# HGRN2 chunk scores: merging two blocks at a time in seven levels in place of four in three

## The chip, the cores and the metric

The kernel runs on one core of a Trainium2 chip. Its engines work side by side, each through its own queue of instructions in a fixed order, and wait for one another by semaphores: TensorE (PE, matrix products, with PEld for the loading of weights), VectorE (DVE, elementwise work), ScalarE (ACT), GpSimd (POOL) and SyncE (SP, which issues the DMAs here). The metric is the device time of one execution in microseconds (us), lower is better. The kernel before takes 2606.49 us, the median of three runs (2604.78 to 2610.13).

## The reference, cut to what matters

The program is a trunk of two layers over 1024 tokens of width 1024: an HGRN2 mixer, a SwiGLU feed-forward, a dilated attention mixer, a second feed-forward, each with a norm and a residual sum, all in float32. The change is in the HGRN2 mixer, in the scores within a chunk. Per head (8 of them, 128 keys each) and chunk the reference computes

```
b      = cumsum(log f, along the chunk)
decay  = exp(where(s <= t, b[t] - b[s], -inf))          # product of f over s+1 .. t
scores = einsum('bhtk,bhsk,bhtsk->bhts', q, k, decay)   # k = 1 - f
o_t    = (q * exp(b)) @ state + scores @ v
state  = exp(b_last) * state + (k * exp(b_last - b)).T @ v
```

The decay depends on t, s and the key, so the scores are not one matrix product of q and k. The kernel takes chunks of 128 tokens and builds the scores from blocks that grow: between two neighbouring blocks, decay splits into a factor of the query (product of f from its block's start up to t) and a factor of the key (product of f behind s up to its block's end), so that q and k, scaled with these, give that block of scores by a plain product. After each step q and k take up the factor of the block they now belong to.

## The kernel before, in words

All tiles have 128 partitions. A head's q, f and k lie with the key index on the partitions and the 1024 tokens along the row, as eight chunks of 128. A projection "unit" (line 130) loads a 128x1024 weight tile, splits it into a high and a low part (ACT copies, line 108, DVE subtracts, line 109), and multiplies both with the split input v in 48 matmuls of 512 columns (lines 124, 125, 127). Each head has four units: f, q, i, g. The loop over heads (near line 423) issues for head j: f and q, the tail of head j-1, i and g, then `hgrn_scores`, then `hgrn_state`, which transposes values and keys (lines 370, 379), carries the state over the chunks (lines 385, 389) and forms the outputs (lines 395, 397). `hgrn_tail` transposes the result back (line 415) and gates it. For the last head the g unit is issued behind the scores.

`hgrn_scores` (line 273) does three things.

- The diagonal (lines 277 to 287): GpSimd multiplies q and k (line 280); `column_sums` (line 265) splits the product and sums it over the partitions by two matmuls with a matrix of ones; DVE writes that, times the identity, to the score tile `at` (line 282). Then `qp` becomes q times f (line 287).
- Three stages with block sizes m of 1, 4 and 16 (`STAGES`, line 29), each in two halves of 512 tokens. Each merges four blocks into one: ACT and DVE form, in `mb`, the six scaled copies of the queries that the six pairs of blocks need (lines 307 to 309); the products follow (for m = 1 through GpSimd multiplies, line 317, and `column_sums`; for 4 and 16 by matmuls of 192 columns, line 327); DVE forms the block products of f (lines 328 to 330), rescales `qp` and `kk` in place (lines 332 to 336), and writes the three diagonals of blocks into `at` by predicated copies under a mask from `lm` (line 342), twelve to a stage.
- A last merge of two blocks of 64 (lines 346 to 361), by matmuls of 128 columns (line 350) and a predicated copy (line 357).

The order of instructions on each engine is set when the program is built: a scheduler interleaves the independent pieces by its own estimates, so that the matmuls of the next head's f and q units stand between the score matmuls of this head. On the chip each engine runs its list in that order. Score results go to four PSUM buffers (`axps`), unit results to four others (`mmps`). A float32 matmul (both operands F32) shows in the profile as two MATMUL instructions, each with its own LDWEIGHTS; one of F32R operands shows as one.

Of the kernel before, what the change touches and what calls it, by code (L numbers as in the profile page):

```python
# [8 lines left out]
F32 = mybir.dt.float32  # L9
F32R = mybir.dt.float32r  # L10
U8 = mybir.dt.uint8
# [4 lines left out]
P = 128  # L16
T = 1024
D = 1024
KT = D // P
# [9 lines left out]
STAGES = (1, 4, 16)  # L29
NMASK = 3 * len(STAGES) + 1  # L30
EPS = 1e-6
# [4 lines left out]
K_ID, K_BAND, K_DIAG, K_COS, K_SIN, K_LM = 0, 128, 384, 512, 1536, 2560  # L36
# [4 lines left out]
def trunk_kernel(ctx, tc, x, cols, consts, w_in, w_hout, w_qkv, w_aout, w_ffn, w_down, out):  # L41
    nc = tc.nc
    cp = ctx.enter_context(tc.tile_pool(name="cp", bufs=1))
# [7 lines left out]
    def big(tag, name, dt=F32):  # L51
        return gp.tile([P, T], dt, tag=tag, name=name, bufs=slots[tag])
# [7 lines left out]
    def axps(name):  # L60
        return pax.tile([P, 512], F32, tag="ax", name=name)

    def hs(hh):
        return slice(hh * 512, hh * 512 + 512)

    def cs(c):
        return slice(c * P, c * P + P)

# [9 lines left out]
    for k in range(KT):  # L78
        t = big("vc", f"x{k}")
# [16 lines left out]
    ones = cp.tile([P, P], F32, name="ones")  # L96
    nc.vector.memset(ones[:], 1.0)
    onesr = cp.tile([P, P], F32R, name="onesr")
    nc.vector.tensor_copy(onesr[:], ones[:])
# [117 lines left out]
    lm = cp.tile([P, NMASK, 2, P], U8, name="lm")  # L217
    for i0 in range(0, NMASK, 8):
        n = min(8, NMASK - i0)
        lmf = big("ws", f"lmf{i0}")  # L220
        nc.sync.dma_start(lmf[:, 0:n * P], consts[:, K_LM + i0 * P:K_LM + (i0 + n) * P])
        for r in range(2):
            nc.vector.tensor_copy(lm[:, i0:i0 + n, r, :], lmf[:, 0:n * P].rearrange("p (i t) -> p i t", i=n))
# [42 lines left out]
    def column_sums(ps, src, hi, lo):  # L266
        nc.scalar.copy(hi, src)
        nc.vector.tensor_sub(lo, src, hi.bitcast(F32))
        nc.tensor.matmul(ps, onesr[:], hi, start=True, stop=False)
        nc.tensor.matmul(ps, onesr[:], lo, start=False, stop=True)  # L270

    def hgrn_scores(j, f, kk, q):
        at = big("ws", f"at{j}")
        qp = big("ws", f"qp{j}")
        tl = big("ws", f"tl{j}")
        for hh in range(2):
            h0 = hh * 512
            ps = axps(f"dg{j}{hh}")
            pr = big("vb", f"pr{j}{hh}", F32R)
            nc.gpsimd.tensor_mul(qp[:, hs(hh)], q[:, hs(hh)], kk[:, hs(hh)])  # L280
            column_sums(ps[:], qp[:, hs(hh)], pr[:, 0:512], pr[:, 512:T])
            nc.vector.tensor_mul(
                at[:, hs(hh)].rearrange("p (c t) -> p c t", c=4),
                ps.rearrange("p (c t) -> p c t", c=4),
                ident.unsqueeze(1).to_broadcast([P, 4, P]),
            )
            nc.vector.tensor_mul(qp[:, hs(hh)], q[:, hs(hh)], f[:, hs(hh)])
        def blocks(ap, n, m):
            return ap.rearrange("p (g b m) -> p g b m", b=n, m=m)

        space = iter([(tl, 0), (f, 0), (f, 256)])
        tot = f[:]
        for si, m in enumerate(STAGES):
            base, at0 = next(space)
            ng = T // (4 * m)
            tt_all = base[:, at0:at0 + 3 * ng].rearrange("p (g b) -> p g b", b=3)
            nxt = base[:, at0 + 3 * ng:at0 + 4 * ng]
            for hh in range(2):
                n2 = ng // 2
                gs = slice(hh * n2, hh * n2 + n2)  # L300
                mb = big("vb", f"mb{j}_{m}_{hh}")
                tv = tot.rearrange("p (g b) -> p g b", b=4)[:, gs, :]
                tt = tt_all[:, gs, :]
                qv = blocks(qp[:, hs(hh)], 4, m)
                kv = blocks(kk[:, hs(hh)], 4, m)
                mv = blocks(mb[:, 0:768], 6, m)
                nc.scalar.copy(mv[:, :, 0:3, :], qv[:, :, 1:4, :])
                nc.vector.tensor_mul(mv[:, :, 3:5, :], qv[:, :, 2:4, :], tv[:, :, 1:3].unsqueeze(3).to_broadcast([P, n2, 2, m]))
                nc.vector.tensor_mul(mv[:, :, 5, :], mv[:, :, 4, :], tv[:, :, 1:2].to_broadcast([P, n2, m]))
                pss = []  # L310
                if m == 1:
                    xp = big("vb", f"xp{j}_{hh}")
                    yh = big("vb", f"yh{j}_{hh}", F32R)
                    yl = big("vb", f"yl{j}_{hh}", F32R)
                    xv = blocks(xp[:, 0:768], 6, m)
                    for a, n in ((0, 3), (3, 2), (5, 1)):
                        nc.gpsimd.tensor_mul(xv[:, :, a:a + n, :], mv[:, :, a:a + n, :], kv[:, :, 0:n, :])
                for b in range(2):
                    ps = axps(f"lv{j}_{m}_{hh}_{b}")
                    pss.append(ps)  # L320
                    if m == 1:
                        sl = slice(b * 384, b * 384 + 384)
                        column_sums(ps[:, 0:384], xp[:, sl], yh[:, sl], yl[:, sl])
                        continue
                    for c in range(2):
                        c4 = 2 * b + c
                        nc.tensor.matmul(ps[:, c * 192:c * 192 + 192], kk[:, hh * 512 + c4 * P:hh * 512 + c4 * P + P], mb[:, c4 * 192:c4 * 192 + 192], start=True, stop=True)  # L327
                nc.vector.tensor_mul(tt[:, :, 1], tv[:, :, 2], tv[:, :, 3])
                nc.vector.tensor_mul(tt[:, :, 0], tv[:, :, 1], tt[:, :, 1])
                nc.vector.tensor_mul(nxt[:, gs], tv[:, :, 0], tt[:, :, 0])  # L330
                t0 = tv[:, :, 0:1].to_broadcast([P, n2, m])
                nc.vector.tensor_mul(qv[:, :, 1, :], qv[:, :, 1, :], t0)
                nc.vector.tensor_mul(qv[:, :, 2, :], mv[:, :, 3, :], t0)
                nc.vector.tensor_mul(qv[:, :, 3, :], mv[:, :, 5, :], t0)
                nc.vector.tensor_mul(kv[:, :, 0:2, :], kv[:, :, 0:2, :], tt[:, :, 0:2].unsqueeze(3).to_broadcast([P, n2, 2, m]))
                nc.vector.tensor_mul(kv[:, :, 2, :], kv[:, :, 2, :], tv[:, :, 3:4].to_broadcast([P, n2, m]))
                for b in range(2):
                    av = blocks(at[:, hh * 512 + b * 256:hh * 512 + b * 256 + 256], 4, m)
                    pv = blocks(pss[b][:, 0:384], 6, m)
                    for d, s0 in ((1, 0), (2, 3), (3, 5)):  # L340
                        mk = blocks(lm[:, 3 * si + d - 1].rearrange("p r t -> p (r t)"), 4, m)
                        nc.vector.copy_predicated(av[:, :, d:4, :], mk[:, :, d:4, :], pv[:, :, s0:s0 + 4 - d, :])  # L342
            tot = nxt
        tv = tot.rearrange("p (g b) -> p g b", b=2)
        nxt = f[:, 320:328]
        for hh in range(2):
            ps = axps(f"lw{j}_{hh}")
            for c in range(4):
                s = slice(hh * 512 + c * P, hh * 512 + c * P + P)
                nc.tensor.matmul(ps[:, cs(c)], kk[:, s], qp[:, s], start=True, stop=True)  # L350
            kv = blocks(kk[:, hs(hh)], 2, 64)
            qv = blocks(qp[:, hs(hh)], 2, 64)
            gs = slice(4 * hh, 4 * hh + 4)
            nc.vector.tensor_mul(kv[:, :, 0, :], kv[:, :, 0, :], tv[:, gs, 1:2].to_broadcast([P, 4, 64]))
            nc.vector.tensor_mul(qv[:, :, 1, :], qv[:, :, 1, :], tv[:, gs, 0:1].to_broadcast([P, 4, 64]))
            nc.vector.tensor_mul(nxt[:, gs], tv[:, gs, 0], tv[:, gs, 1])
            nc.vector.copy_predicated(
                at[:, hs(hh)].rearrange("p (c t) -> p c t", c=4),
                lm[:, NMASK - 1, 0].unsqueeze(1).to_broadcast([P, 4, P]),
                ps.rearrange("p (c t) -> p c t", c=4),  # L360
            )
        tot = nxt
        return kk, qp, at, tot
# [57 lines left out]
    for j in range(H):  # L421
        f, kk, q = hgrn_fq(j)
        if pend is not None:
            os_.append(hgrn_tail(*pend))
        if j == H - 1:
            vt = scaled(unit(w_in[2 * H + j], v, f"i{j}"), "wx", f"i{j}")
            sc = hgrn_scores(j, f, kk, q)
            g = gated(j, 3 * H, "g")
        else:
            vt, g = hgrn_ig(j)  # L430
# [335 lines left out]
    for j in range(4):  # L766
        st = sp.tile([P, 3, 8, 2], F32, tag="st", name=f"st{j}", bufs=2)
        os3 = []
        for gi in range(3):
            blocks, place = attn_scores(j, gi, st)  # L770
# [124 lines left out]
```

## Time and profile before

| | before |
|---|---|
| median of 3 runs | 2606.49 us (2604.78 to 2610.13) |
| profiled execution, first to last instruction (span) | 2605.1 us; the page gives no other time of this execution |
| PE busy | 2546.4 us, 98% |
| PEld busy | 2118.4 us, 81% |
| DVE busy | 1732.1 us, 66% |
| ACT busy | 785.1 us, 30% |
| POOL busy | 129.9 us, 5% |
| DMA | 215 MB, mean 83 GB/s |

The busy share counts an instruction from its start to its end. Matmuls are pipelined: the next one starts before the last has ended, so the time that a matmul takes up on PE is the distance from one start to the next, which is shorter than its duration. The chain of waits, which follows the work that ended last, gives these distances. HGRN2 fills the first 530 us or so; one head follows the other every 62 us.

### The profile page before, as it was taken

To read this page: it belongs to the slowest core of one execution; us is meant where nothing else is said; L and a number is where in the kernel's file an instruction comes from. 1 tells how busy PE (TensorE), PEld (TensorE's weight loads), DVE (VectorE), ACT (ScalarE), POOL (GpSimd) and SP (SyncE) were. 2 spreads that over 40 slices of the span, in tenths; PEclk is the share of its full clock that TensorE was granted. 3 is DMA by queue.
4 is the path that set the end of the run, shared out by engine and by line. 5 is a ranking of instruction groups with operands and counts; after the bars stand their busy time and mean duration, and the time that the engine had idled before them with its cause. 6 is when DMAs were issued, how large, how long until landed. Compare 5 with 4: busy or idle time off the path is not lost.

```text
span 2605.1 us, 30351 instructions
## 1 busy us (share of the span) xinstructions
PE 2546.4 (98%) x12044; PEld 2118.4 (81%) x12044; DVE 1732.1 (66%) x2957; ACT 785.1 (30%) x1168; POOL 129.9 (5%) x107
## 2 busy tenths in 40 slices
PE   8999999999999999999999999999999999999998
PEld 6888888788888888888887878787878888888887
DVE  8888888977777777433545464636377777775336
ACT  5222222344323233212231313134242323333212
POOL 1111111111000000000000000000010000000000
PEclk9999999999999999999999999999999999999999
DMA  3101111142222224531211121213322222236323
GB/s 144 33 33 33 33 33 33 44 143 89 79 84 80 89 81 149 183 100 61 97 41 58 41 58 41 61 34 101 115 81 89 81 89 81 81 102 229 110 58 127
DMA packets 77518, 215.24 MB, mean 83 GB/s; under 512 B 21696, under 2 KB 24000, under 8 KB 77376
## 3 DMA queue, kind: packets, MB, share of 16 engines
q1 hardware_dynamic: 77376, 213.30, 25.3%
q8 instruction: 95, 1.56, 0.2%
q14 instruction: 47, 0.39, 0.0%
HBM read 173.28 MB, written 39.99 MB: 82 GB/s over the span
## 4 chain that ended last, share of the span: by engine, by line
PE 81%; DVE 11%; DMA 3%; issue 2%; ACT 1%; POOL 1%; SPq 0%; POOLq 0%; DVEq 0%; ACTq 0%
PE pt L483 6%; PE pt L482 6%; PE pt L481 6%; PE pfw L125 6%; PE pfw L127 6%; PE pfw L124 6%; PE pb L482 4%; PE pb L483 4%; PE pb L481 4%; PE p_n L125 2%; PE p_n L124 2%; PE p_n L127 2%; PE lv L327 2%; PE as L670 1%; PE p_aq L127 1%
## 5 line engine op out<-in xcount | busy, mean ns | idle before, releaser
L563 DVE TENSOR_TENSOR h<-pfw,h 128x512 f32<-128x512 f32 (+1 forms) x104 | 63.6, 646 | 217.6 <-PE pfw L127 217.5
L108 ACT CAST h_fw<-r_fw 128x896 fp32r<-128x896 f32 (+1 forms) x60 | 58.3, 973 | 249.7 <-PE pfw L125 206.4
L108 ACT CAST h_fa<-r_fg 128x1024 fp32r<-128x1024 f32 x44 | 46.4, 1056 | 198.4 <-PE pt L482 183.5
L108 ACT CAST h_fb<-s 128x1024 fp32r<-128x1024 f32 x44 | 46.4, 1054 | 171.1 <-PE pb L482 159.6
L342 DVE COPY_PREDICATED at<-lm,lv 128x192 f32<-128x192 uint8 (+2 forms) x288 | 82.2, 353 | 4.0 <-PE lv L327 3.2
L677 ACT ACTIVATE ap<-ap,ng 128x256 f32<-128x256 f32 (+1 forms) x96 | 41.9, 438 | 124.4 <-DVE ng L675 124.4
L156 POOL TENSOR_TENSOR rs_n<-ms_n,half 128x8 f32<-128x8 f32 (+2 forms) x7 | 9.0, 1281 | 1353.8 <-DVE ms_n L154 1353.8
L494 DVE TENSOR_TENSOR s<-r_fu 128x512 f32<-128x512 f32 x44 | 30.3, 691 | 65.8 <-DMA r_fu<-in_w_ffn_dram 65.7
L482 PE MATMUL pb<-n3b,h_fa 128*128 128x512 f32 x176 | 68.7, 390 | 2.6 <-DVE n3b L456 2.6
L109 DVE TENSOR_TENSOR l_fw<-r_fw,h_fw 128x896 fp32r<-128x896 f32 (+1 forms) x60 | 67.1, 1121 | 4.6 <-ACT h_fw L108 4.0
L482 PE MATMUL pb<-n1b,h_fa 128*128 128x512 f32 x176 | 68.6, 390 | 1.2 <-DVE n1b L456 1.2
L481 PE MATMUL pb<-n3b,h_fa 128*128 128x512 f32 x176 | 68.8, 391 | 0.5 <-ACT n3b L455 0.5
L481 PE MATMUL pt<-n3t,h_fb 128*128 128x512 f32 x176 | 68.6, 390 | 0.0
L481 PE MATMUL pt<-n1t,h_fb 128*128 128x512 f32 x176 | 68.6, 390 | 0.0
L481 PE MATMUL pb<-n1b,h_fa 128*128 128x512 f32 x176 | 68.6, 390 | 0.0
L483 PE MATMUL pb<-n3b,l_fa 128*128 128x512 f32 x176 | 68.5, 389 | 0.0
L482 PE MATMUL pt<-n3t,h_fb 128*128 128x512 f32 x176 | 68.5, 389 | 0.0
L483 PE MATMUL pb<-n1b,l_fa 128*128 128x512 f32 x176 | 68.5, 389 | 0.0
L483 PE MATMUL pt<-n1t,l_fb 128*128 128x512 f32 x176 | 68.5, 389 | 0.0
L483 PE MATMUL pt<-n3t,l_fb 128*128 128x512 f32 x176 | 68.5, 389 | 0.0
L482 PE MATMUL pt<-n1t,h_fb 128*128 128x512 f32 x176 | 68.5, 389 | 0.0
L517 DVE TENSOR_TENSOR t<-pt,t 128x512 f32<-128x512 f32 x44 | 30.4, 691 | 51.0 <-PE pt L483 50.9
(1036 smaller groups left out, 7840.3 us busy)
## 6 DMA issues: line engine op xcount, KB each, us to landing
r_fu<-in_w_ffn_dram SPq DMA_DIRECT2D x44, 512.0 KB, 3.6
r_fg<-in_w_ffn_dram SPq DMA_DIRECT2D x44, 512.0 KB, 3.6
act<-g SPq DMA_DIRECT2D x44, 512.0 KB, 2.6
st<-act SPq DMA_DIRECT2D x44, 512.0 KB, 4.3
r_fw<-in_w_down_dram SPq DMA_DIRECT2D x44, 448.0 KB, 3.4
h<-hd SPq DMA_DIRECT2D x16, 512.0 KB, 5.5
r_fw<-in_w_down_dram SPq DMA_DIRECT2D x16, 512.0 KB, 3.6
r_aq<-in_w_qkv_dram SPq DMA_DIRECT2D x12, 512.0 KB, 3.6
```

The lines of the kernel that those rows point to most:

```text
L108: nc.scalar.copy(hi[:, a:b], src[:, a:b])
L109: nc.vector.tensor_sub(lo[:, a:b], src[:, a:b], hi[:, a:b].bitcast(F32))
L124: nc.tensor.matmul(p[:, 0:b - a], wh, vh[:, a:b], start=(first and i == 0), stop=False)
L125: nc.tensor.matmul(p[:, 0:b - a], wh, vl[:, a:b], start=False, stop=False)
L127: nc.tensor.matmul(p[:, 0:b - a], wl, vh[:, a:b], start=False, stop=(last and i == n - 1))
L327: nc.tensor.matmul(ps[:, c * 192:c * 192 + 192], kk[:, hh * 512 + c4 * P:hh * 512 + c4 * P + P], mb[:, c4 * 192:c4 * 192 + 192], start=Tru ...
L342: nc.vector.copy_predicated(av[:, :, d:4, :], mk[:, :, d:4, :], pv[:, :, s0:s0 + 4 - d, :])
L481: nc.tensor.matmul(ps[:], wh, bh, start=(kk == 0), stop=False)
L482: nc.tensor.matmul(ps[:], wh, bl, start=False, stop=False)
L483: nc.tensor.matmul(ps[:], wl, bh, start=False, stop=(kk == 3))
L563: nc.vector.tensor_add(h[d][:, a:b], ps[i][:, 0:b - a], h[d][:, a:b])
L677: nc.scalar.activation(place[b], place[b], AF.Exp, bias=ng[:, b:b + 1], scale=SCALE, accum_out=st[:, gi, b, 1:2])
```

## The change

The scores within a chunk now go through seven levels, m = 1, 2, 4, ..., 64, and each merges two blocks into one, over all 1024 tokens at once. A level has eight matmuls of 64 columns (one for each chunk: all keys of the chunk against the queries of its odd blocks, read with a stride), one rescaling of those queries and one of the keys of the even blocks, one product of the block totals, and one move of the result into `at`: a predicated copy for m below 32, and ACT copies (two for m = 32, one for m = 64) that need no mask. The tile `mb` with the six copies, `column_sums`, the ones in F32R and every GpSimd multiply of this function are gone. The diagonal is now the plain product of k and q, eight float32 matmuls of 128 columns, times the identity. `qp` is q times f in one instruction of 1024 columns in place of two of 512. Five masks of 128 columns are loaded by five DMAs and cast by one DVE instruction; before it was ten masks, two DMAs and four casts. The block totals lie in `tl` and no longer in parts of `f`.

```diff
-STAGES = (1, 4, 16)
+STAGES = (1, 2, 4, 8, 16)
...
-    onesr = cp.tile([P, P], F32R, name="onesr")
-    nc.vector.tensor_copy(onesr[:], ones[:])
...
-    lm = cp.tile([P, NMASK, 2, P], U8, name="lm")
...
+    lm = cp.tile([P, len(STAGES), P], U8, name="lm")
+    lmf = big("ws", "lmf")
+    for si in range(len(STAGES)):
+        nc.sync.dma_start(lmf[:, cs(si)], consts[:, K_LM + 3 * si * P:K_LM + (3 * si + 1) * P])
+    nc.vector.tensor_copy(lm[:], lmf[:, 0:len(STAGES) * P].rearrange("p (i t) -> p i t", i=len(STAGES)))
...
-    def column_sums(ps, src, hi, lo):
...
     def hgrn_scores(j, f, kk, q):
         at = big("ws", f"at{j}")
         qp = big("ws", f"qp{j}")
         tl = big("ws", f"tl{j}")
+        nc.vector.tensor_mul(qp[:], q[:], f[:])
...
-            nc.gpsimd.tensor_mul(qp[:, hs(hh)], q[:, hs(hh)], kk[:, hs(hh)])
-            column_sums(ps[:], qp[:, hs(hh)], pr[:, 0:512], pr[:, 512:T])
+            for c in range(4):
+                s = slice(hh * 512 + c * P, hh * 512 + c * P + P)
+                nc.tensor.matmul(ps[:, cs(c)], kk[:, s], q[:, s], start=True, stop=True)
             nc.vector.tensor_mul(
                 at[:, hs(hh)].rearrange("p (c t) -> p c t", c=4),
...
-            nc.vector.tensor_mul(qp[:, hs(hh)], q[:, hs(hh)], f[:, hs(hh)])
...
         tot = f[:]
-        for si, m in enumerate(STAGES):
...
+        at0 = 0
+        for si in range(7):
+            m = 1 << si
+            n = T // (2 * m)
+            tv = tot.rearrange("p (g b) -> p g b", b=2)
+            qv = qp.rearrange("p (g b m) -> p g b m", b=2, m=m)
+            kv = kk.rearrange("p (g b m) -> p g b m", b=2, m=m)
+            ps = axps(f"lv{j}_{m}")
+            ng = 64 // m
+            for c in range(KT):
+                nc.tensor.matmul(ps[:, c * 64:c * 64 + 64], kk[:, cs(c)], qv[:, c * ng:c * ng + ng, 1, :], start=True, stop=True)
+            nc.vector.tensor_mul(qv[:, :, 1, :], qv[:, :, 1, :], tv[:, :, 0:1].to_broadcast([P, n, m]))
+            nc.vector.tensor_mul(kv[:, :, 0, :], kv[:, :, 0, :], tv[:, :, 1:2].to_broadcast([P, n, m]))
+            nxt = tl[:, at0:at0 + n]
+            at0 += n
+            nc.vector.tensor_mul(nxt, tv[:, :, 0], tv[:, :, 1])
+            av = at.rearrange("p (c g b m) -> p c g b m", c=KT, b=2, m=m)
+            pv = ps.rearrange("p (c g m) -> p c g m", c=KT, m=m)
+            if m < 32:
+                mk = lm[:, si].rearrange("p (g b m) -> p g b m", b=2, m=m)[:, :, 1, :]
+                nc.vector.copy_predicated(av[:, :, :, 1, :], mk.unsqueeze(1).to_broadcast([P, KT, ng, m]), pv)
+            else:
+                for g in range(ng):
+                    rows = slice(2 * g * m, 2 * g * m + m)
+                    nc.scalar.copy(av[rows, :, g, 1, :], pv[rows, :, g, :])
             tot = nxt
```

On PE in the second head, before, the first stage of four blocks of size 4 stands in two groups with one matmul of the next head's f unit between them (`lv_4_0` and `lv_4_1` are the two halves, `kk` the keys, `mb` the scaled queries, `p_f` the next unit):

```order
502 L327 MATMUL lv_4_0_0_1111<-mb_4_0_1107,kk_820 128x192 [waits DVE_49,PE_49,Activation_49]
503 L327 MATMUL lv_4_0_0_1111<-mb_4_0_1107,kk_820 128x192
504 L327 MATMUL lv_4_0_1_1114<-mb_4_0_1107,kk_820 128x192 [waits PE_49]
505 L327 MATMUL lv_4_0_1_1114<-mb_4_0_1107,kk_820 128x192
506 L124 MATMUL p_f_1_1304<-v_5h,h_f_1299 128x512
507 L327 MATMUL lv_4_1_0_1135<-mb_4_1_1131,kk_820 128x192 [waits DVE_49,PE_49,Activation_49]
508 L327 MATMUL lv_4_1_0_1135<-mb_4_1_1131,kk_820 128x192
509 L327 MATMUL lv_4_1_1_1138<-mb_4_1_1131,kk_820 128x192 [waits PE_49]
510 L327 MATMUL lv_4_1_1_1138<-mb_4_1_1131,kk_820 128x192
```

The changed kernel has on PE at the same place, still in the second head, level 4 and then level 8, with seven matmuls of the f unit between them (`lv_4` and `lv_8` are the levels):

```order
475 L288 MATMUL lv_4_962<-qp_921,kk_722 128x64 [waits DVE_49,PE_49]
476 L288 MATMUL lv_4_962<-qp_921,kk_722 128x64 x7
477 L125 MATMUL p_f_1_1111<-v_3h,l_f_1107 128x512
478 L122 MATMUL p_f_0_1110<-v_4h,h_f_1106 128x512
479 L123 MATMUL p_f_0_1110<-v_4l,h_f_1106 128x512
480 L122 MATMUL p_f_1_1111<-v_4h,h_f_1106 128x512
481 L123 MATMUL p_f_1_1111<-v_4l,h_f_1106 128x512
482 L125 MATMUL p_f_0_1110<-v_4h,l_f_1107 128x512
483 L125 MATMUL p_f_1_1111<-v_4h,l_f_1107 128x512
484 L288 MATMUL lv_8_975<-qp_921,kk_722 128x64 [waits DVE_49,PE_49]
485 L288 MATMUL lv_8_975<-qp_921,kk_722 128x64 x7
```

The rows 506, and 477 to 483, are what PE does between two pieces of the scores; at this place it went from one matmul to seven.

On DVE the changed kernel has, in the same head, from the end of level 1 to the end of level 4 (`l_i` is the low part of the weights of the next head's i unit, `tl` the block totals, `at` the scores):

```order
119 L290 TENSOR_TENSOR kk_722<-kk_722,f_717 128x512
120 L298 COPY_PREDICATED at_920<-lm,lv_1_936 128x512 [waits DVE_49]
121 L293 TENSOR_TENSOR tl_922<-tl_922 128x256
122 L107 TENSOR_TENSOR l_i_1245<-r_i_1242,h_i_1244 128x1024 [waits DMAHW3_49]
123 L289 TENSOR_TENSOR qp_921<-qp_921,tl_922 128x256x2 [waits DVE_49,PE_49]
124 L290 TENSOR_TENSOR kk_722<-kk_722,tl_922 128x256x2 [waits DVE_49]
125 L298 COPY_PREDICATED at_920<-lm,lv_2_949 128x256x2 [waits DVE_49]
126 L293 TENSOR_TENSOR tl_922<-tl_922 128x128 [waits DVE_49]
127 L293 TENSOR_TENSOR tl_922<-tl_922 128x64 [waits DVE_49]
128 L293 TENSOR_TENSOR tl_922<-tl_922 128x32 [waits DVE_49]
129 L289 TENSOR_TENSOR qp_921<-qp_921,tl_922 128x128x4 [waits PE_49]
130 L290 TENSOR_TENSOR kk_722<-kk_722,tl_922 128x128x4
```

The pair of rescalings (rows 123 and 124, 129 and 130) waits for the level's matmuls and is what the next level's matmuls wait for; the predicated copy of the level before stands ahead of it in DVE's queue.

## Rows read from the trace of the kernel before

**Rows 1.** The page, part 1: busy us, share of the span, instructions.

```profile
PE 2546.4 (98%) x12044; PEld 2118.4 (81%) x12044; DVE 1732.1 (66%) x2957; ACT 785.1 (30%) x1168; POOL 129.9 (5%) x107
```

**Rows 2.** Busy time of each engine in single heads, with PE's granted clock.

```profile
core 0: us, PE busy (x) PEld busy (x) DVE busy (x) ACT busy (x) POOL busy (x), PEclk, DMA share, GB/s
161.42:223.12 61.70, 61.31 (x323) 52.23 (x321) 55.08 (x146) 16.68 (x26) 12.44 (x10) 1.00 0.11 35
...
408.23:472.02 63.79, 61.65 (x323) 52.04 (x321) 53.37 (x146) 16.68 (x26) 12.01 (x10) 1.00 0.11 34
472.02:540.00 67.98, 60.70 (x299) 49.22 (x298) 61.72 (x152) 23.51 (x33) 13.37 (x10) 0.97 0.15 47
```

**Rows 3.** The chain of waits in one head: start us, us it took up, what.

```profile
138.41 0.23 PE p_q L124
...
139.09 1.30 PE lv L327 x8
...
142.15 0.89 PE lw L350 x8
...
144.86 0.87 PE vp L370 x8
...
150.06 0.22 PE kv L385 x2
150.28 0.22 PE op L397 x2
```

**Rows 4.** Timeline of PE, third head: start us, duration, what, idle before.

```profile
184.25 0.34 PE L269 MATMUL lv<-yh,onesr 128*128 128x384 f32 x1
...
184.78 0.34 PE L270 MATMUL lv<-yl,onesr 128*128 128x384 f32 x1
...
193.51 1.54 PE L327 MATMUL lv<-mb,kk 128*128 128x192 f32 x8 [0.38 <-DVE f L329]
```

**Rows 5.** Single lines of the kernel: durations in ns, min/median/max, heads 1 to 7.

```profile
L350 PEld LDWEIGHTS lw<-qp,kk x112: 186/192/192, 80.1 to 455.7; 128*128 128x128 f32 x112
L350 PE MATMUL lw<-qp,kk x112: 271/275/347, 80.2 to 455.9; 128*128 128x128 f32 x112
...
L370 PEld LDWEIGHTS vp<-kon,i x56: 138/140/144, 82.7 to 457.1; 128*128 128x128 f32 x56
```

**Rows 6.** Timeline of PE in the last feed-forward, F32R matmuls of 256 columns.

```profile
2560.09 0.28 PE L127 MATMUL pfw<-ac_20h,l_fw 128*128 128x256 f32 x1
2560.21 0.28 PE L124 MATMUL pfw<-ac_21h,h_fw 128*128 128x256 f32 x1
```

**Rows 7.** Waits of PE from 425 to 450 us: total, times, longest.

```profile
PE lv L269 <- ACT yh L267: 1.9, 1, 1.9
```

**Rows 8.** Timeline of PE in the last head's scores, with idle time in brackets.

```profile
485.46 0.86 PE L269 MATMUL lv<-yh,onesr 128*128 128x384 f32 x2 [1.32 <-ACT yh L267]
...
494.37 0.44 PE L269 MATMUL lv<-yh,onesr 128*128 128x384 f32 x1 [1.96 <-ACT yh L267]
...
507.06 3.17 PE L327 MATMUL lv<-mb,kk 128*128 128x192 f32 x16 [1.59 <-DVE f L329]
```

**Rows 9.** Timeline of DVE in two heads: start us, duration, what.

```profile
183.28 1.29 DVE L244 TENSOR_TENSOR g<-p_g,rb_n 128x512 f32<-128x512 f32 x2 [0.30 <-PE p_g L127]
...
188.21 0.41 DVE L335 TENSOR_TENSOR kk<-kk,tl 128x256 f32<-128x256 f32 x1
188.54 0.73 DVE L342 COPY_PREDICATED at<-lm,lv 128x64 f32<-128x64 uint8 x2
...
195.45 0.28 DVE L336 TENSOR_TENSOR kk<-kk,tl 128x128 f32<-128x128 f32 x1
195.65 0.50 DVE L342 COPY_PREDICATED at<-lm,lv 128x64 f32<-128x64 uint8 x2
...
206.64 0.73 DVE L357 COPY_PREDICATED at<-lm,lw 128x512 f32<-128x512 uint8 x1
...
484.70 0.38 DVE L336 TENSOR_TENSOR kk<-kk,f 128x128 f32<-128x128 f32 x1
```

**Rows 10.** The costliest groups of the first 520 us, each shape apart.

```profile
L156 POOL TENSOR_TENSOR rs_o<-ms_o,half 128x4 f32<-128x4 f32 x14 | 20.5, 1461 | 264.1 <-DVE ms_o L154 264.1
```

More of the change, by code (lines that the diff above doesn't have):

```diff
@@ L215, in trunk_kernel @@
         rb = nm.finish("vb")
-    lm = cp.tile([P, NMASK, 2, P], U8, name="lm")
[L218 to L223, printed above, removed]
+    lm = cp.tile([P, len(STAGES), P], U8, name="lm")
[3 more added lines that the diff above has]
+    nc.vector.tensor_copy(lm[:], lmf[:, 0:len(STAGES) * P].rearrange("p (i t) -> p i t", i=len(STAGES)))
     lg = col[:, C_LB:C_LB + 24]
@@ L264, in hgrn_ig @@
         return vt, gated(j, 3 * H, "g")
-    def column_sums(ps, src, hi, lo):
[L267 to L270, printed above, removed]
     def hgrn_scores(j, f, kk, q):
@@ L275, in hgrn_scores @@
         tl = big("ws", f"tl{j}")
+        nc.vector.tensor_mul(qp[:], q[:], f[:])
         for hh in range(2):
-            h0 = hh * 512
             ps = axps(f"dg{j}{hh}")
-            pr = big("vb", f"pr{j}{hh}", F32R)
-            nc.gpsimd.tensor_mul(qp[:, hs(hh)], q[:, hs(hh)], kk[:, hs(hh)])
-            column_sums(ps[:], qp[:, hs(hh)], pr[:, 0:512], pr[:, 512:T])
+            for c in range(4):
+                s = slice(hh * 512 + c * P, hh * 512 + c * P + P)
+                nc.tensor.matmul(ps[:, cs(c)], kk[:, s], q[:, s], start=True, stop=True)
             nc.vector.tensor_mul(
@@ L286, in hgrn_scores @@
             )
-            nc.vector.tensor_mul(qp[:, hs(hh)], q[:, hs(hh)], f[:, hs(hh)])
-        def blocks(ap, n, m):
-            return ap.rearrange("p (g b m) -> p g b m", b=n, m=m)
-        space = iter([(tl, 0), (f, 0), (f, 256)])
         tot = f[:]
-        for si, m in enumerate(STAGES):
[L294 to L342, printed above, removed]
-            tot = nxt
@@ L344, in hgrn_scores @@
[L344 to L361, printed above, removed]
@@ L362, in hgrn_scores @@
-        tot = nxt
+        at0 = 0
[23 more added lines that the diff above has]
+                    nc.scalar.copy(av[rows, :, g, 1, :], pv[rows, :, g, :])
+            tot = nxt
```

## The prediction

> **What bounds the kernel now.** I read the page's busy shares first: PE is busy for 98% of the span, DVE for 66% [rows 1]. A busy share counts matmuls from start to end, and these overlap, so it doesn't prove that PE has no room. I therefore went to the HGRN2 stage, the only one that the change touches, and cut it by heads: a middle head lasts 61.70 us, with PE busy for 61.31 and DVE for 55.08; POOL for 12.44 [rows 2]. The chain of waits then gives what a matmul takes up: 0.23 us for one F32R matmul of 512 columns, 1.30 for eight float32 instructions of 192 columns (0.1625 each), 0.89 for eight of 128 columns (0.111), 0.87 for eight transposes (0.109), 0.11 for one instruction of the state's products [rows 3]; the F32R ones of 384 columns start 0.177 apart (three steps from 184.25 to 184.78) [rows 4].
>
> With these I add up PE's work in a head: four units of 48 matmuls at 0.227 (the mean of 0.23 and the shorter ones) make 43.5 us; the scores 9.3 (below); 23 transposes 2.5; 44 instructions of state and output products 4.8. That is 60.1 of the 61.7 us. PE's work is the bound of a middle head, with 1.6 us of waits, of which 0.38 stands in the trace at the first matmul of stage m = 4, behind DVE [rows 4]. DVE and POOL are covered there. So what counts is PE time, and DVE or POOL time only where PE waits for it.
>
> **The change part by part.** Scores on PE, per head, before: diagonal 4 x 0.23 = 0.9; m = 1, 8 x 0.177 = 1.4; stages 4 and 16, 16 matmuls = 32 instructions x 0.1625 = 5.2; last merge 16 x 0.111 = 1.8; sum 9.3 us [rows 3, 4].
>
> After: the diagonal has 8 float32 matmuls, 16 instructions x 0.111 = 1.8. The levels have 7 x 8 matmuls, 112 instructions of 64 columns, a size that the trace doesn't hold. From below: 192 and 128 columns differ by 0.0515, 0.8 ns a column, which continued to 64 gives 0.060, so 6.7 us. From above: if loading its weights stood bare before each, the load's full 0.192 [rows 5], so 21.5. In between: each of the 112 loads 128 x 128 float32 weights, as the 128-column ones do, and there the load already seems to be what limits: the plain products start 0.111 apart with loads of 192 ns, the transposes, as many columns, 0.109 apart with loads of 140 [rows 3, 5]; and F32R matmuls of 256 columns, half as long on PE as those of 512, start 0.12 apart [rows 6]. I take 0.111, the nearest row in weights: 12.4 us. With the diagonal 14.2, so **+4.9 us of PE work a head**; the ends give -0.8 and +14, and 0.12 gives +5.9.
>
> The Trainium skill, TensorE: Matmul & The Clock Gate, section LDWEIGHTS, says that a load takes its column count over 1.2 GHz, whatever the rows: 107 ns here, and that would make 12.0 us of the levels. The same page's section Back-to-back issue gap has a table by which a matmul of up to 64 columns takes some 60 cycles, 25 ns; by that the levels would be 2.8 us. The trace has nothing under 0.109 for float32, which stands with the first.
>
> DVE: the levels have fourteen 512-element products, seven products of totals, five predicated copies of 512. Two 512-element products in a row take 1.29 us [rows 9]. Between a level and the next PE has seven f-unit matmuls, 7 x 0.227 = 1.59 us, more in the first two gaps (13 and 10). DVE needs the end of the last level matmul (0.275 after its start, 0.111 of which PE itself uses [rows 5]) plus 1.29: 1.45 us and the hand-overs. It fits barely, so no wait to speak of; if the two products were 0.1 slower, PE would wait 0.1 at each level.
>
> Level 1 and 2 read with strides. Stride 4 costs: 128 elements at stride 4 take 0.38, dense 0.28; but pairs out of four (256 elements in 0.41) cost as dense [rows 9]. Level 1 has stride 2, between the two; if it cost as stride 4, three products before level 2 (totals, qp, kk) would each be 0.4 longer. The lead there, from the order: the first level ends 3.6 us after the diagonal's start and 13 matmuls follow, until 6.5; DVE has g's scaling, two diagonal writes, totals, g's gate and the two products, seven times 0.6 and one of twice that, plus a wait for the sigmoid, done at about 5.8. So 0.7 is free of 1.2: at worst 0.5 a head. The predicated copy at m = 1: before, 64 elements with stride 4 took 0.36, with runs of 16 0.25 [rows 9]; the 512-element one lies between 0.73 and 2.9, eight times 0.36. It stands before level 2's rescaling in DVE's queue, behind it a product of totals and the split of the next i weights; the room, counted as before, is 1.3 over the 0.73, so at worst 0.9 of PE waiting a head, 1.7 if the reads before it are late as well. I take 0 for both, since the strided reads meet two of every four elements, like the pairs.
>
> The Trainium skill, SBUF — State Buffer, section Door 1, speaks of 16-byte lines that give full rate when met at least twice, up to a stride of four float32. The trace agrees for pairs (0.41) and not for stride 4 (0.38 against 0.28); stride 2 meets each line twice and would cost nothing more.
>
> What goes: twelve small predicated copies to a stage, ACT's copies and splits, all of POOL's multiplies. In a middle head PE's own work covers them; with them goes the wait of 0.38 before m = 4 [rows 4], and I take 0.45 of the 1.6 us. What is late next is PE itself. The seventh and the last head are different. In the seventh (408 to 472) PE waited 1.9 for ACT behind the split of the m = 1 products [rows 7], and the head is 2.1 longer [rows 2]. In the last, where only the g unit stands beside the scores, PE waited 1.32, 1.96 and 1.59 for the same path and for DVE [rows 8], and the granted clock there is 0.97 of 68 us, as from two us lost to a stretch at the lower level [rows 2]: 6.9 in all. After, that head has eight to ten matmuls of g between its levels, more than DVE needs, so I take all 9 us as gained. On the other side, its two output halves are now normed as a pair, with two GpSimd powers of 1.46 us [rows 10] in a row before the first transpose back: 1 us more (0 to 3).
>
> Masks: five loads in place of two on SP's queue, in front of the weights of the first i unit, which are due more than 20 us later: nothing.
>
> Sum: seven heads x (4.9 - 0.45) = 31.2; seventh head -2.1; last head 4.9 - 6.9 + 1 = -1.0. Together **+28 us**. The profiled execution's span is 2605.1 us, 1.4 less than the median of the runs, which I leave as a fixed rest: 2606.5 + 28 = 2634.5, say 2634.
>
> **Rivals.**
>
> A, cost by columns: a 64-column float32 instruction takes 0.060. For it: 192 and 128 columns differ just by columns, and the second of the two rules of the page on TensorE goes that way, further still. Against: the loads, as above. Then a head is -0.8 - 0.45, so seven make -8.8; -2.1; last head -0.8 - 6.9 + 1 = -6.7. 2606.5 - 17.6 = 2589, faster. It decides below about 0.08 per instruction: at 0.08 the levels take 9.0, +1.5 a head, 7.4 - 2.1 - 4.4 = +1, no change (2607).
>
> B, DVE in the first two levels: stride costs the worst in both places, 2.2 us a head, 17.6 in all: 2652. For it: the 0.38 against 0.28. Against: the pairs.
>
> C, bare loads: 0.192 per instruction, +14 - 0.45 a head: 2606.5 + 95 - 2 + 8 = 2708. Against it: the 128-column matmuls overlap their loads already.
>
> D, that the stage isn't bound by PE but by DVE or POOL, and the relief there pays in each head: the most it could give is the 1.6 us of waits, less than the 4.9; so it doesn't turn the sign unless A holds too.
>
> **How the numbers follow.** The forecast 0.60, B 0.20, A 0.11, the 0.08 case 0.05, C 0.04. What a measurement of this kernel can tell from no change is about 0.2%, 5 us. Slower by more: 0.60 + 0.20 + 0.04 = 0.84; same 0.05; faster 0.11. The range: down to 2606, where a cost per instruction of 0.08 and no stride cost ends, up to 2658, B with most of the 8 that 0.12 per instruction would add. A and C lie outside, 0.15.
>
> **What would show it.** Right: starts of 64-column matmuls 0.11 apart; middle heads of 66 us; PE idle in the last head's scores gone and its clock full; DVE busy in a head down by a third or more; POOL left with the powers. Wrong: starts 0.06 apart and heads of 60 us (A); PE waiting for DVE at level 2 or 4 in every head (B). It would also be wrong if the scheduler's gaps are too short at all seven levels, with PE waiting at each.

## The result, and the profile after

The changed kernel takes 2635.53 us (median of four runs, 2633.76 to 2637.16), the kernel before 2608.01 (2604.78 to 2610.13) on the same chip: a ratio of 1.0103, with a 95% interval of 1.0089 to 1.0117. That is 27.5 us slower; the forecast was 28 slower. The profiled execution has a span of 2632.6 us, also 27.5 more than before.

The busy line of the page answers to [rows 1]: GpSimd has lost its products, DVE has 140 us less, PE has 37.5 us more.

```profile
PE 2583.9 (98%) x12588; PEld 2161.3 (82%) x12588; DVE 1592.0 (60%) x2273; ACT 745.2 (28%) x1096; POOL 48.0 (2%) x43
```

The same cut by heads as [rows 2] (columns as there): the third head, the seventh, and the last up to 570 us.

```profile
core 0: us, PE busy (x) PEld busy (x) DVE busy (x) ACT busy (x) POOL busy (x), PEclk, DMA share, GB/s
171.57:237.63 66.06, 66.06 (x390) 57.27 (x389) 37.13 (x61) 11.66 (x17) 1.98 (x2) 1.00 0.10 32
435.83:501.90 66.07, 66.07 (x390) 57.29 (x389) 37.14 (x61) 11.67 (x17) 1.98 (x2) 1.00 0.11 33
501.90:570.00 68.10, 67.02 (x393) 57.99 (x392) 46.30 (x70) 21.46 (x28) 1.98 (x2) 1.00 0.22 70
```

A middle head takes 66.06 us in place of 61.70, and PE is busy in all of it, while DVE falls by a third, from 55.08 to 37.13 us. The chain of waits in that head, which answers to [rows 3], gives the prices:

```profile
193.62 1.78 PE dg L271 x16
...
207.67 1.79 PE lv L288 x16
209.46 0.28 PE p_f L122
...
218.04 1.77 PE lv L288 x16
219.81 0.88 PE vp L311 x8
```

Sixteen instructions of 64 columns take 1.79 us, 0.112 each, as much as sixteen of 128 columns (the diagonal, 1.78). Between two levels the timeline of PE and DVE (start us, duration, what, idle before) shows who waits:

```profile
206.05 0.69 DVE L289 TENSOR_TENSOR qp<-qp,tl 128x512 f32<-128x512 f32 x1 [0.99 <-PE lv L288]
206.37 0.39 PE L123 MATMUL p_f<-v_4l,h_f 128*128 128x512 f32 x1
206.60 0.39 PE L122 MATMUL p_f<-v_4h,h_f 128*128 128x512 f32 x1
206.66 0.69 DVE L290 TENSOR_TENSOR kk<-kk,tl 128x512 f32<-128x512 f32 x1
206.83 0.39 PE L123 MATMUL p_f<-v_4l,h_f 128*128 128x512 f32 x1
207.06 0.62 PE L125 MATMUL p_f<-v_4h,l_f 128*128 128x512 f32 x2
207.26 0.71 DVE L298 COPY_PREDICATED at<-lm,lv 128x512 f32<-128x512 uint8 x1
207.51 1.96 PE L288 MATMUL lv<-qp,kk 128*128 128x64 f32 x16
...
209.50 0.69 DVE L289 TENSOR_TENSOR qp<-qp,tl 128x512 f32<-128x512 f32 x1 [1.27 <-PE lv L288]
```

DVE waits for PE at five of the head's seven levels (0.99 and 1.27 us here, 5.7 in all); PE has no idle time in front of the level. The rescaled keys are ready at 206.66 + 0.69 = 207.35, the next level starts at 207.51: 0.16 us to spare. In heads 2 to 7 the list of PE's waits is empty; before it held 1.9 us there for ACT's split at m = 1, in one place, and 1.7 us for DVE at the next stages, in five. The last head had 3.3 and 1.6 us of these two before and has neither now.

By stretches, between the first matmuls of the units in the two traces (us):

| stretch | before | after | difference | forecast |
|---|---|---|---|---|
| start to the first i unit | 36.78 | 39.57 | +2.8 | 0 |
| head 1 | 62.93 | 65.94 | +3.0 | +4.45 |
| heads 2 to 6 | 308.51 | 330.31 | +21.8 | +22.25 |
| head 7 | 63.79 | 66.07 | +2.3 | +2.35 |
| last head, to the first feed-forward matmul | 138.53 | 132.71 | -5.8 | -1.0 |
| feed-forward 1 and the attention units | 692.01 | 692.08 | +0.1 | 0 |
| attention scores to the last matmul, the second feed-forward included | 1295.68 | 1299.12 | +3.4 | 0 |

### The profile page after: what moved, and what is told of

Read it like the earlier page. It is cut to its first block, busy times and chain, and to the rows that moved or that the text cites. A ratio compares the mean times of both kernels' runs of the same rounds, so it can differ in the third digit from the quotient of the medians.

```text
span 2632.6 us, 30587 instructions
## 1 busy us (share of the span) xinstructions
PE 2583.9 (98%) x12588; PEld 2161.3 (82%) x12588; DVE 1592.0 (60%) x2273; ACT 745.2 (28%) x1096; POOL 48.0 (2%) x43
## 3 DMA queue, kind: packets, MB, share of 16 engines
q8 instruction: 99, 1.62, 0.3%
## 4 chain that ended last, share of the span: by engine, by line
PE 87%; DVE 7%; DMA 3%; issue 2%; ACT 1%; POOL 0%; SPq 0%; POOLq 0%; DVEq 0%; ACTq 0%
PE pt L422 6%; PE pt L424 6%; PE pt L423 6%; PE pfw L123 6%; PE pfw L125 6%; PE pfw L122 5%; PE pb L423 4%; PE pb L424 4%; PE pb L422 4%; PE lv L288 4%; PE p_n L122 2%; PE p_n L123 2%; PE p_n L125 2%; PE as L611 1%; PE p_aq L125 1%
## 5 line engine op out<-in xcount | busy, mean ns | idle before, releaser
L288 PEld LDWEIGHTS lv<-qp,kk 128*128 128x128 f32 x896 | 105.8, 192 | 7.7 <-issue 6.1
L288 PE MATMUL lv<-qp,kk 128*128 128x64 f32 x896 | 107.4, 272 | 0.0
L435 DVE TENSOR_TENSOR s<-r_fu 128x512 f32<-128x512 f32 x44 | 30.3, 691 | 63.5 <-DMA r_fu<-in_w_ffn_dram 63.5
```

The source lines that it names most:

```text
L288: nc.tensor.matmul(ps[:, c * 64:c * 64 + 64], kk[:, cs(c)], qv[:, c * ng:c * ng + ng, 1, :], start=True, stop=True)
```

## The experiments

Each time is a median, with its ratio to runs of the kernel before on the same chip and the 95% interval.

| run | us | ratio | interval |
|---|---|---|---|
| 1 fewer weights | 2626.34 | 1.0072 | 1.0058 to 1.0086 |
| 2 fewer moving columns | 2633.78 | 1.0102 | 1.0085 to 1.0119 |
| 3 diagonal alone | 2661.16 | 1.0202 | 1.0182 to 1.0222 |
| 4 no copies | 2634.55 | 1.0101 | 1.0086 to 1.0117 |
| 5 diagonal, q times f first | 2616.23 | 1.0026 | 1.0017 to 1.0035 |
| 6 small last merge | 2607.26 | 0.9997 | 0.9988 to 1.0006 |
| 7 both schemes | 2603.25 | 0.9981 | 0.9972 to 0.9990 |
| 8 more DVE | 2637.06 | 1.0108 | 1.0095 to 1.0122 |
| 9 last head alone | 2606.26 | 0.9989 | 0.9978 to 1.0000 |
| 10 both schemes, 96 weights | 2602.15 | 0.9980 | 0.9971 to 0.9989 |

**1. Fewer weights in the last two levels.**

```
-  nc.tensor.matmul(ps[:, c * 64:c * 64 + 64], kk[:, cs(c)], qv[...], ...)
+  w = P - m if m >= 32 else P
+  nc.tensor.matmul(ps[0:w, c * 64:c * 64 + 64], kk[:, c * P:c * P + w], qv[...], ...)
```

> The changed kernel, but the last two levels load only the weights that they need: 64 columns at m = 64, 96 at m = 32, in place of 128; the moving 64 columns stay. Theory (a 64-column float32 instruction takes as long as its weight load): 0.1115 us falls to about 0.056 at m = 64 and to about 0.083 at m = 32, in proportion to the weights. 16 x 0.056 + 16 x 0.028 = 1.35 us a head, 10.8 in eight: 2635.5 - 10.8 = 2625. Rival 1 (a fixed price of about 0.11 for any float32 instruction, whatever it loads): no change, 2635. Rival 2 (PE isn't what the levels wait for, DVE is): PE's starts come closer, but the time doesn't move, 2635.

Measured: 2626.3. The chain of one head (levels m = 16, 32, 64):

```profile
275.00 1.77 PE lv L289 x16
...
278.45 1.34 PE lv L289 x16
...
281.47 1.08 PE lv L289 x16
282.55 1.02 PE vp L312 x8
```

With 96 weight columns sixteen instructions take 1.34 us (0.085 apart), with 64 they take 1.08; inside that group they start 0.058 apart, which would make 0.93; 0.15 is lost at its ends, and 0.14 in the transposes behind it (1.02 against 0.88). The head falls from 66.07 to 65.04 us, 8.2 in eight heads. The theory holds, and rivals 1 and 2 fall: the price follows the weights, and the time follows PE.

**2. Fewer moving columns.** At m = 64 the 32 columns are the first of the 64; the copies into `at` are halved as well.

```
-  ..., kk[:, cs(c)], qv[:, c * ng:c * ng + ng, 1, :], ...
+  ..., kk[:, cs(c)], qv[:, c * ng:c * ng + ng // 2, 1, :], ...
```

> The changed kernel, but each level's matmul moves 32 columns in place of 64 past the same 128 weight columns; the other half of each level's pairs is left out, and its copies too. Theory (weight load): starts stay 0.11 apart, the time stays at 2635, within 3 us. Rival A (cost by columns, on top of a small fixed part): 0.0515 us for 64 columns less per 192 to 128, so 32 columns would save 0.026 an instruction, 112 x 0.026 x 8 = 23 us: 2612; in full proportion 50 us: 2585.

Measured: 2633.8, and in the chain a level of half the columns takes what a whole one takes:

```profile
201.10 1.70 PE lv L289 x16
202.81 0.32 PE p_f L123
```

With the matmul behind it that is 2.02 us, against 1.79 + 0.28 = 2.07 for 64 columns. Halving the columns saves next to nothing, and rival A falls. Together with the first run: a small float32 instruction of this kernel costs its weight load.

**3. The diagonal alone.** A miss by 47 us.

```
-  nc.gpsimd.tensor_mul(qp[:, hs(hh)], q[:, hs(hh)], kk[:, hs(hh)])
-  column_sums(ps[:], qp[:, hs(hh)], pr[:, 0:512], pr[:, 512:T])
+  for c in range(4):
+      nc.tensor.matmul(ps[:, cs(c)], kk[:, s], q[:, s], start=True, stop=True)
```

> The kernel before, with the diagonal alone made a plain product of eight matmuls (16 instructions of 128 columns) in place of GpSimd's product, the split and four F32R matmuls. Theory (the price is PE's): 16 x 0.1115 - 4 x 0.232 = +0.86 us a head, 6.9 in eight; the last head may lose the wait of 1.5 us ahead of m = 1: 2608 + 6 = 2614, range 2611 to 2616. Rival (what counts is GpSimd's and ACT's part in the chain to m = 1): the waits in the seventh and the last head go with the diagonal, 2 + 3 us, and the time is 2608 + 7 - 5 = 2610 or less.

Measured: 2661.2. Heads 2 to 7 take 67.8 to 70.2 us, with 22.0 us of waits for ACT's split at m = 1 in eleven places from 100 to 515 us. The timeline of one head:

```profile
334.72 1.95 PE L281 MATMUL dg<-q,kk 128*128 128x128 f32 x16
335.89 0.68 DVE L282 TENSOR_TENSOR at<-dg,kon 128x512 f32<-128x512 f32 x1
336.49 0.68 DVE L287 TENSOR_TENSOR qp<-q,f 128x512 f32<-128x512 f32 x1
...
337.94 1.43 POOL L317 TENSOR_TENSOR xp<-mb,kk 128x384 f32<-128x384 f32 x1 [22.99 <-issue]
...
342.43 0.93 ACT L267 CAST yh<-xp 128x384 fp32r<-128x384 f32 x2 [4.62 <-POOL xp L317]
...
343.00 0.44 PE L269 MATMUL lv<-yh,onesr 128*128 128x384 f32 x1 [1.56 <-ACT yh L267]
```

The product of q and f now stood on DVE behind the write of the diagonal, which waits for PE; so GpSimd's products for m = 1 began after the diagonal, in place of during the units of i and g (before, in the third head, they run from 170.65 to 179 us and the diagonal's matmuls start at 183.32), and PE waited at m = 1 twice a head. I had costed the edit and not read its order on DVE.

**5. The diagonal alone, with q times f ahead of it.**

```
+  nc.vector.tensor_mul(qp[:], q[:], f[:])
   for hh in range(2):
       ps = axps(f"dg{j}{hh}")
```

> As in the run with the diagonal alone, but the product of q and f, with which the chain of m = 1 (ACT's copy, GpSimd's products, the split) begins, stands ahead of the diagonal in the program, so that it doesn't queue on DVE behind a write that waits for PE's diagonal. Theory (the diagonal's price is 0.86 us of PE a head; the 55 us of the run before came from the order, PE waiting for a chain that began too late): 2607 + 7 = 2614, range 2610 to 2617, and no idle time of 2 us ahead of the matmuls of m = 1. Rival (GpSimd's and ACT's chain of m = 1 is slower for another reason, as that it now shares its operands with PE): still 2650 or more.

Measured: 2616.2, as expected; 45 us of the miss came from the order. The product now starts 18 us ahead of the diagonal:

```profile
295.88 1.22 DVE L276 TENSOR_TENSOR qp<-q,f 128x1024 f32<-128x1024 f32 x1
...
313.81 1.95 PE L282 MATMUL dg<-q,kk 128*128 128x128 f32 x16
```

PE's waits from 100 to 515 us (who waits for whom: us in total, times, longest) have no line for ACT's split any more:

```profile
PE lv L327 <- DVE f L328: 2.9, 6, 0.5
PE lv L269 <- DVE at L283: 2.8, 2, 2.6
PE op L397 <- DVE sst L389: 2.4, 6, 0.4
```

A middle head takes 63.5 us, 1.8 more than before, of which the diagonal's own matmuls are 0.77 (1.70 against 0.93). Another 0.5 is idle time of PE (0.88 a head against 0.39), as in the waits above; the last 0.5 isn't traced here. The last head is 2.4 shorter. In the changed kernel, where PE has no such waits, the diagonal takes 0.85 more a head (1.78 against 0.93): by its matmuls it is some 7 of the 27 us.

**4. No copies.**

```
-  nc.vector.copy_predicated(av[:, :, :, 1, :], mk.unsqueeze(1).to_broadcast(...), pv)
+  pass
```

> The changed kernel without the five predicated copies of the levels m = 1 to 16, so that those levels' scores don't reach the score tile; all matmuls and rescalings stay. It takes 0.71 to 1.31 us five times a head off DVE. Theory (in every level PE comes to the next level after DVE is done, 0.17 us and more after): no change, 2633 to 2636. Rival B (DVE's strided work sets the pace of the first levels): 0.3 us or more a level, five levels, eight heads: 12 us or more off, 2623 or less.

**8. More DVE.**

```
+  nc.vector.tensor_mul(qv[:, :, 1, :], qv[:, :, 1, :], ones[:, 0:1]...to_broadcast([P, n, m]))
   nc.vector.tensor_mul(kv[:, :, 0, :], kv[:, :, 0, :], tv[:, :, 1:2]...)
```

> The changed kernel with one product more on DVE at each level, a multiplication by one of 512 elements (0.6 us) ahead of the rescaling of the keys, on which the next level's matmuls wait. The program's own order then places 9 to 10 unit matmuls between two levels in place of 7. Theory (PE has other work to put between the levels, DVE isn't the bound): no change, 2633 to 2639. Rival D (DVE's chain sets the pace): 0.6 x 7 levels x 8 heads = 34 us more, 2669. In between, if the order leaves DVE late by some 0.4 at four levels: 2649.

Measured: 2634.6 and 2637.1. One middle head of each, without the copies and with more products:

```profile
238.10:304.20 66.10, 66.10 (x391) 57.05 (x389) 33.21 (x56) 11.54 (x17) 1.98 (x2) 1.00 0.11 33
```

```profile
240.72:307.26 66.54, 66.40 (x390) 57.30 (x389) 41.18 (x69) 11.76 (x16) 1.98 (x2) 1.00 0.10 32
```

DVE's work goes from 33.21 to 41.18 us a head, the head by 0.4. Rivals B and D fall. The extra product came behind the keys' rescaling in DVE's queue, not ahead of it, but still ahead of the next level, which needs both. That PE's list of waits stays almost empty (one of 0.2 us, at a transpose) is the order's doing: 9 to 10 unit matmuls stand between the later levels, where 7 stood. Had the order stayed, 0.6 would have met 0.16 to spare.

**6. The kernel before with a small last merge.** A miss. A plain copy replaces the predicated one, and two masks more are loaded, which only runs 7, 9 and 10 use.

```
-  nc.tensor.matmul(ps[:, cs(c)], kk[:, s], qp[:, s], ...)
+  nc.tensor.matmul(ps[0:64, c * 64:c * 64 + 64], kk[:, s:s + 64], qp[:, s + 64:s + P], ...)
```

> The kernel before, but its last merge loads only the 64 weight columns that it needs, moves 64 columns, and is written by a plain copy. Theory (load by columns): 16 instructions at 0.056 in place of 0.1115, 0.89 us a head, 7.1 in eight: 2607 - 7 = 2600. Rival (what PE gains there comes back as waits for DVE behind m = 16): 2605 or more.

Measured: 2607.3, no change. The rival named waits; in the middle heads the chain shows something else:

```profile
267.79 0.61 PE lw L350 x8
268.40 0.43 PE p_q L127
268.83 0.23 PE p_q L124
```

A group of eight takes 0.61 in place of 0.89 [rows 3], but the unit matmul behind it 0.43, where the chain of before has, behind its group of eight:

```profile
143.04 0.23 PE p_q L127
```

That leaves 0.08 a group, 0.16 a head: a middle head went from 61.70 to 61.58. In the sixth head the rival has a part: it takes 62.66 us in place of 61.65, and PE idles 0.5 us each at an output product and at the transposes back, both times for DVE, where it had no wait before. Runs 7 and 10 show the same two waits.

**7. Both schemes**: heads 1 to 7 as in run 6, the last in seven levels with the weights of run 1.

```
   if j == H - 1:
-      sc = hgrn_scores(j, f, kk, q)
+      sc = hgrn_levels(j, f, kk, q)      # the function of the changed kernel
```

> Heads one to seven as in the run with the small last merge, the last head in seven levels with fewer weights at the last two. Theory: 7 x 0.89 = 6.2 us less in the seven heads; in the last head 131.7 us to the first matmul of the feed-forward part, as in the run with fewer weights, in place of 138.5, so 6.8 less: 2607 - 13 = 2594, range 2590 to 2599. Rival (the seam between the two schemes, where the seventh head already waits 2 us for ACT, costs as much as the last head gives): 2600.

Measured: 2603.3, a miss by 9 us. The last head takes 131.73 us as expected, and the seam costs nothing (the seventh head takes 63.72 us, 63.79 before), so the rival falls too; the 6.2 us of the seven others are missing, as in run 6.

**9. The last head alone**: the same edit on the kernel before, nothing else.

> The kernel before, with the seven levels and the plain diagonal in the last head alone. Theory (there PE waits for GpSimd, ACT and DVE, and the levels, between which unit matmuls stand, do away with that): the last head takes 132.7 us to the first matmul of the feed-forward part, as in the changed kernel, in place of 138.5: 2607.5 - 5.8 = 2602, range 2598 to 2606. Rival (the 5.8 us come from the six heads ahead, whose scheme leaves less work over for the last): the last head stays at 137 or more, the time at 2606 or more.

Measured: 2606.3, just above the range; the ratio's interval touches 1, so a gain in time isn't shown. The last head does take 132.68 us, so the rival falls. In the profiled execution, the slowest of the eleven (2609.95), other stretches ate it: 39.32 us to the first i unit (36.78 before), 63.63 in head 1 (62.93), 64.75 in head 7 (63.79), and 1299.73 from the attention scores on (1295.68). The first isn't the edit's: up to the first i unit runs 6, 7 and 10 have the same instructions in the same order as this one, and take 38.69, 38.01 and 36.59. Which of the others belong to the kernel is open. The waits of PE in the last head shrink from seven lines with 7.1 us to one:

```profile
PE ot L459 <- DVE on L447: 1.0, 1, 1.0
```

**10. As run 7, with 96 weights in the small merge.**

```
-  nc.tensor.matmul(ps[0:64, ...], kk[:, s:s + 64], ...)
+  nc.tensor.matmul(ps[0:96, ...], kk[:, s:s + 96], ...)
```

> As the run that joined the two schemes, but the small last merge of heads one to seven loads 96 weight columns in place of 64. Theory (what ate half of the gain of 64 columns is a price of some 0.25 us at each group, on the matmuls at its two ends, which the 96-column group of the changed kernel with fewer weights did not show): 16 x 0.0265 = 0.42 us a head kept in full, in a middle head 61.3 us in place of 61.58; the time 2601, range 2597 to 2605. Rival (the gain goes to waits for DVE and ACT at the end of the scores, whatever the load): middle heads stay at 61.6 us, the time at 2603 or more.

Measured: 2602.2, and 61.37 us for a middle head, where run 7 has 61.58. The two runs' times, 1.1 us apart, don't tell them apart, but in the heads more weights are faster here:

```profile
202.95 0.65 PE lw L350 x8
203.60 0.28 PE p_q L127
203.88 0.23 PE p_q L124
```

0.65 + 0.28 = 0.93 against 0.61 + 0.43 = 1.04 with 64 weights and 0.89 + 0.23 = 1.12 with 128. Two groups a head: 0.38 less than before, close to the 0.33 seen. This kernel beats both, by 0.2% and 1.3%.

## Why the prediction was right

**PE bounds the middle heads: right.** PE's wait list is empty there, and runs 4 and 8, whose DVE work lies 8 us a head apart, differ by 0.4 us a head. The working had 1.6 us of waits in a head before, by its sum; PE's idle time there is 0.39 (61.70 less 61.31). From start to start the four units take 46.2 us with it, in place of the 43.5 of the sum: a unit's matmul behind a group of small ones takes longer (0.28 in the chain above, 0.23 in [rows 3]).

**0.111 per 64-column instruction: right**, at a median of 0.112 at each of the seven levels; rival C's 0.192 falls with it. The nearest row in weights was the right one to follow; the line through 192 and 128 columns was not, since 128, 64 and 32 columns all start 0.112 apart (run 2).

The Trainium skill, TensorE: Matmul & The Clock Gate, section LDWEIGHTS, has a load take its columns over 1.2 GHz: 107, 80 and 53 ns for 128, 96 and 64. Measured starts are 112, 85 and 58 apart, 5 above each, so the trace agrees in the slope. The table in that page's section Back-to-back issue gap is for a single matmul and leaves the load out, as the page says itself, so it couldn't be the price of this stream: with 32 moving columns the starts stay at 112.

**The scores' sum: right.** Forecast 9.3 to 14.2 us a head; from start to start the trace has 8.90 (diagonal 0.93, stages 6.35, last merge 1.62) and 13.91 (1.78 and 12.13). The +5.0 stands against +4.9. The rest of a middle head gave back 0.65, not 0.45; 0.39 of it is PE's idle time. Heads of 66.06 us against 66.

**Head 7, -2.1: right.** The wait for ACT is gone, 2.3 more where 2.35 were said. Head 1 rose by only 3.0: before, it had lasted 62.93, 1.2 more than the next ones, which I hadn't looked at.

**Strides at nothing: right in effect.** The stride-2 products take the same 0.69 us as dense ones. The copy I had at 0.73 takes 1.31 and 1.30 at m = 1 and 2 and 0.71 at m = 4:

```profile
198.85 1.31 DVE L298 COPY_PREDICATED at<-lm,lv 128x512 f32<-128x512 uint8 x1
...
203.17 1.30 DVE L298 COPY_PREDICATED at<-lm,lv 128x512 f32<-128x512 uint8 x1
```

The room of 1.3 us over 0.73 that I had counted held it, and taking the copies away gains nothing (run 4).

**The last head, -1.0: the mis-sized term.** It measured -5.8. The step that failed was "6.9 in all": I added the three longest waits and the clock up to 540 us. From start to start, to the first feed-forward matmul, the last head's diagonal, stages and merge took 12.65 us where a middle head's take 8.90 (3.75 of waits), the g unit 3.07 more than after, the output projection 2.3 and the transposes and state products 1.5 more: 10.6. Nor did the tail cost 1 us: the two powers take 1.0 each (1.98 for both in the last head's row above), not 1.46, a mean of 1.91 beside a DVE split and 1.01 without, and PE waits 1.0 at one transpose group where it waited 1.1 at two.

```profile
L154 POOL TENSOR_TENSOR rs_o<-ms_o,half 128x4 f32<-128x4 f32 x14 | 13.9, 1007 | 449.5 <-DVE ms_o L152 449.5
```

**Masks at nothing: wrong by about 1 us.** What they cost isn't the loads, but DVE's order. The start of the kernel, before:

```profile
31.25 0.28 DVE L223 CAST lm<-lmf 128x256 uint8<-128x256 f32 x1
31.41 1.64 POOL L156 TENSOR_TENSOR rs_n<-ms_n,half 128x8 f32<-128x8 f32 x1 [30.97 <-DVE ms_n L154]
31.56 1.21 DVE L109 TENSOR_TENSOR l_i<-r_i,h_i 128x1024 fp32r<-128x1024 f32 x1
...
33.11 1.09 PE L187 MATMUL rt_n<-kon,rs_n 128*128 128x128 f32 x8 [1.28 <-POOL rs_n L156]
```

And in the changed trace:

```profile
31.71 1.23 DVE L107 TENSOR_TENSOR l_g<-r_g,h_g 128x1024 fp32r<-128x1024 f32 x1
31.88 2.56 POOL L154 TENSOR_TENSOR rs_n<-ms_n,half 128x8 f32<-128x8 f32 x1 [31.43 <-DVE ms_n L152]
...
34.49 1.82 PE L185 MATMUL rt_n<-kon,rs_n 128*128 128x128 f32 x8 [1.98 <-POOL rs_n L154]
```

The short casts of the masks that stood on DVE when GpSimd's first power began are gone; a split of 1.23 us stands there, and the power takes 2.56 us in place of 1.64. All five kernels with the change's mask code show 2.56, the seven others 1.64 or 1.75. PE idles 1.98 us in place of 1.28. The whole start takes 39.6 to 41.1 us in the five traces and 36.6 to 39.3 in the seven, so a part of the 2.8 between the two kernels' traces can be chance.

**The rest that wasn't forecast** is clock. Behind that idle time the granted clock shows its lower level (1.2 GHz) for 3.4 us, as it does in two of the other four traces with the idle time of 1.98 and in none of the seven without:

```profile
34.60:38.10 3.50, 3.50 (x13) 3.11 (x14) 1.67 (x5) 1.46 (x4) 0.00 (x0) 0.51 0.33 125
```

At half the clock for 3.4 us such a stretch costs 1.7 us, by estimate. The last row of the table has 3.4 us of it before and 10.2 after, by which it would last 3.4 longer; its idle time on PE is the same (29.9 and 30.0 us), and PE's busy time rises by 3.4 (1265.8 to 1269.2). In the twelve traces of this case that part, which no edit touched, lasts from 1292.7 to 1302.2 us, with none to four such stretches, and traces with one alone from 1293.3 to 1297.5, so other things move it too. I don't put these differences down to the change, and nothing here shows what sets them.

So 28 against 27.5 is partly luck: heads 2 to 7, 24.1 where 24.6 were forecast, are the mechanism; the last head's 4.8 and the first's 1.5 too much were paid back by 2.8 at the start and 3.4 from the attention scores on.

## What to carry to other kernels

A small float32 matmul is priced by the columns of weights it loads, not by the columns it moves: 64 or 32 moving columns cost what 128 do, so cut the weights or give each load more to move, as stages of four blocks did here with 192. Count an engine's relief as a gain only where PE waits for it: 18 us of DVE and 10 of GpSimd a head were worth 0.65 at most. And read the order after an edit: in run 3 one product that slid behind a wait on DVE cost 45 us, where the edit itself cost 8 (run 5).

## What the runs showed of the hardware that was not expected

- Groups of 64-column weights among 128-column ones pay at their ends: the group of eight at 0.058 apart takes 0.61 us and the next matmul 0.43; 96-column weights (0.085 apart) pay hardly any of it, 0.65 and 0.28. The Trainium skill, TensorEngine Tiling (Array Packing), section Key Properties, says that a change of tiling mode drains TensorE; 128 x 64 is a mode in that page's list, 96 columns is none. The numbers fit, with about 0.3 us a group, half of it on the matmul behind, but no run shows that 64 weight columns set that mode.
- A GpSimd power that begins just behind a two-input DVE product takes 0.9 us longer. In the heads of the kernel before, nine of sixteen powers begin 0.17 us behind a split of 1.22 us and take 1.91, the seven others take 1.01; at the start it is 2.56 against 1.64. In the third head, before:

```profile
215.94 1.91 POOL L156 TENSOR_TENSOR rs_o<-ms_o,half 128x4 f32<-128x4 f32 x1 [36.95 <-DVE ms_o L154]
219.55 1.01 POOL L156 TENSOR_TENSOR rs_o<-ms_o,half 128x4 f32<-128x4 f32 x1 [1.70 <-DVE ms_o L154]
```

  The Trainium skill, SBUF — State Buffer, section SBUF: two separate sides, describes an exclusive lock on a port pair that the two share: whichever starts first has it for its whole instruction, and the other waits. The trace fits where DVE is first. Where the power is first it doesn't: the split that begins at 31.56, 0.15 us behind the power's start, takes 1.21 us, as long as elsewhere.
- A predicated copy of 512 elements takes 1.31 us with runs of one or two elements, 0.71 with runs of four and more.
